# Four inner pairs instead of three in the gate_up groups of a fused encoder layer, with four raw buffers, five weight places and the residual's memory for summed blocks

## The chip, the cores and the metric

One core of a Trainium2 chip runs the whole layer as one program. The metric is the device time of one execution in microseconds (us). TensorE (PE) multiplies, VectorE (DVE) and ScalarE (ACT) prepare operands and finish results, GpSimd (POOL) and SyncE (SP) issue the DMAs; SP's queue and POOL's queue are each worked off in order.

## The reference, cut to what matters

```python
def swiglu(h, w_gate_up, w_down):
    gate, up = jnp.split(h @ w_gate_up, 2, axis=-1)
    return (jax.nn.silu(gate) * up) @ w_down

def reference(...):                      # x: 1 x 256 x 2048, float32; DEPTH = 1, D_FF = 5632
    ...                                  # four mixers side by side, w_out; x = x + mix @ w_out
    x = x + cross_attention(rms_norm(x, norm_g[l, 1]), mem_n, w_xq[l], w_xkv[l], w_xo[l])
    x = x + swiglu(rms_norm(x, norm_g[l, 2]), w_gate_up[l], w_down[l])
    return rms_norm(x, final_norm_g)
```

Everything is float32. The change lies in `swiglu`: h is 256 x 2048, `w_gate_up` 2048 x 11264, `w_down` 5632 x 2048.

## The kernel before, in words

**Products.** Each float32 operand is split into a high and a low part. A 128 x 512 block of a product is three matmuls (`part`, L430 to L434): high by high, high by low, low by high.

**The weight stream.** All weights lie in DRAM in the order in which they are used, as slabs of 1 MB (`Stream`). `_load` (L94) brings a slab into one of three raw buffers by a DMA on SP. `_half` (L112) turns half a slab (1024 columns) into a pair `wh`, `wl`: ACT casts (L135), DVE subtracts (L136). A pair takes a place (`_buffers`, L88): three places in pool `wp`, and a fourth, `extra`, over most of the program. `_fill` (L166) prepares as many halves ahead of TensorE as there are places.

**Normal and paired slabs.** A normal slab (N) is four steps of 128 inner rows by 512 columns, for two row blocks of the activations: 24 matmuls of 128 x 512. A paired slab (S) holds 256 inner rows by 1024 columns and does them with seven products instead of eight (`paired_rows`, `take_sums`): 21 matmuls. For that, two inner blocks of the activations are combined once (`combine`, into a tile `z`), and the weights are prepared in four pieces (`_sums`, L140): 1024 columns, 512, a summed block of 1024, 1024. DVE adds raw blocks for the last two (L158). In gate_up the summed block `two` is made partly by DMA: two loads of 256 KB on SP (L101) and one of 512 KB on POOL that adds on arrival (L102); then DVE has two adds of 512 columns left.

**The gate_up stage.** `gate_up` (L1047) walks over 11 groups of 512 hidden columns of gate and of up. Group 0 has eight normal slabs, in which the last blocks of h arrive and the combinations are made. Groups 1 to 10 follow the plan `NNSNSNSN`. After the last S of a group, `mixed` and `gated` read four and two PSUM banks; at the group's end `upped` reads the last two and `up` multiplies by the gate (L1060), transposes (L557) and stores the block to DRAM through POOL (L559). All eight banks are used by a group and pass to the next.

**Background work.** `Background` (L204) is a planner: at each step of TensorE's program, `poll` lets a waiting generator go on if its due time has come and the estimated DVE work that is owed is under 0.9 us. `fetch` (L1087) is one of these: it loads the stored hidden blocks k back from DRAM, turned (L564 on POOL, into the 11 tiles of pool `tmp`), and splits each into a tile `f[k]` (L290 on ACT, L282 on DVE). `early` is the fetch of blocks 0 to 21, begun in group 1; the rest follow after the stage. `bg.drain(early)` (L1135) puts down whatever of it is left before `down` begins. `down` (L1138) starts with four normal slabs, which use `f[12]` to `f[27]` in that order, and then alternates with paired slabs.

The framework puts the instructions of each engine into one fixed order when the program is built; each engine then works through its list in that order.

Of the kernel before, what the change touches and what calls it, by code (L numbers as in the profile page):

```python
# [13 lines left out]
F32 = mybir.dt.float32  # L14
F32R = mybir.dt.float32r
# [8 lines left out]
P = 128  # L24
R = 256
# [24 lines left out]
PAIRED = {a + i for a, plan in [(GATE_UP + 8 * j, GROUP) for j in range(10)] + [(DOWN, PASSES[0]), (DOWN + 22, PASSES[1])]  # L50
          for i, x in enumerate(plan) if x == "S"}
SUMMED = {i for i in PAIRED if i < DOWN}

# [18 lines left out]
class Stream:  # L72


    def __init__(self, tc, pools, W, bg):
        self.tc, self.nc, self.W, self.bg = tc, tc.nc, W, bg
        self.rawp, self.wp = pools
        self.order = []
        self.n = self.made = 0
        self.after = []  # L80
        self.halves = []
        self.at = self.phase = 0
        self.raw = None
        self.extra = self.sums = None
        self.places = []
        self.two = []

    def _buffers(self, n, m):  # L88
# [77 lines left out]
    def _fill(self):  # L166

        ahead = self.at + 1 + min(3 if self.extra else 2, self.n // 16)
        while len(self.halves) < ahead and self.made < NBLK:
            self._half()  # L170

    def _used(self):
# [81 lines left out]
class Block:  # L254
    def __init__(self, ctx, tc, t):
        self.ctx, self.tc, self.nc, self.t = ctx, tc, tc.nc, t
        pool = lambda n, b, **kw: ctx.enter_context(tc.tile_pool(name=n, bufs=b, **kw))
        self.cp = pool("cp", 1)
        self.tp = pool("tp", 11)
        self.rp = pool("rp", 3)  # L260
        self.psG = pool("psG", 4, space=PSUM)
        self.psM = pool("psM", 4, space=PSUM)
        rawp = pool("rawp", 3)
        wp = pool("wp", 3)
        self.bg = Background()
        self.st = Stream(tc, (rawp, wp), t["W"], self.bg)
        self.kept = itertools.count()
        self.run()

# [193 lines left out]
    def paired_rows(self, w, cols, slots, sums, plan, mixed, first, ready=None, late=0, before=None, swap=False):  # L463
# [23 lines left out]
        for i, kind in enumerate(plan):  # L487
            if before:
                before(i)
            if kind == "S":  # L490
                ks, z = next(todo)
# [75 lines left out]
    def run(self):  # L567
# [20 lines left out]
        self.ff = self.outside("hidden", FT)  # L588
        self.gk = [nc.dram_tensor(f"state{i}", (R, P), F32, kind="Internal").ap() for i in range(4)]
        self.vd = nc.dram_tensor("values", (P, 8 * 512), F32, kind="Internal").ap()  # L590
        def load(src, k, n):
# [16 lines left out]
        nc.scalar.copy(self.identr, self.ident)  # L608
        with self.tc.tile_pool(name="wx", bufs=1) as st.extra:
            self.attention(self.mixers())  # L610
# [199 lines left out]
    def half(self, c, r):  # L810

        return self.res[c].rearrange("p k r -> p (k r)")[:, r * 512:(r + 1) * 512]

    def turned(self, to, c, r, x):
# [52 lines left out]
    def attention(self, ps):  # L867
        tc, nc, act, st = self.tc, self.nc, self.act, self.st
        with tc.tile_pool(name="atp", bufs=1) as atp, tc.tile_pool(name="kp", bufs=1) as kp, \
# [109 lines left out]
            self.add_rows(1, 2, self.gemm_rows("w_xo", [1024], o)[0])  # L979
            late.append(self.bg.add(self.arrive(self.xf[1], 2, self.tmp, self.put3, FAR), go=True))  # L980
            st.extra = None
            self.add_rows(1, 3, self.gemm_rows("w_xo", [1536], o)[0])
            for g in late[:2]:
                self.bg.drain(g)
# [44 lines left out]
    def mlp(self):  # L1029
        tc, nc, act = self.tc, self.nc, self.act  # L1030
        with tc.tile_pool(name="fp", bufs=1) as fp:
            self.gap(fp, 192)
            f = [fp.tile([P, 512], F32R, name=f"f{i}") for i in range(14)]
            z = [fp.tile([P, 1024], F32R, name=f"z{i}") for i in range(3)]
            f = act[4:12] + f + [z[i // 2][:, i % 2 * 512:i % 2 * 512 + 512] for i in range(6)] + self.h3
            with tc.tile_pool(name="wy", bufs=1) as self.st.extra:
                self.gap(self.st.extra, 64)
                with tc.tile_pool(name="tw", bufs=2) as self.st.sums, tc.tile_pool(name="gp", bufs=1) as gp:
                    self.gate_up(gp, f, z)
# [7 lines left out]
    def gate_up(self, gp, f, z):  # L1047
# [65 lines left out]

        arrival = lambda: gp.tile([P, R], F32, name="ar", tag="ar", bufs=4)
# [9 lines left out]
        comb = self.bg.add(combined())  # L1124
        ps = self.gemm_rows("w_gate_up", [0, DFF], self.h3,
                            parts=[(range(8), [0]), (range(8, 12), [0]), (range(12), [1]), (range(12, 16), [0]), (range(12, 16), [1])],
                            before=lambda n: n in (1, 3) and self.bg.drain(self.late if n == 1 else last))
        self.bg.drain(col)
        gate(ps[0])
        up(0, ps[1])  # L1130
        early = self.bg.add(fetch(0, FT - 22, 3, 2.0, 15))
        self.bg.drain(comb)
        for j in range(1, DFF // 512):
            upped(j, self.paired_rows("w_gate_up", [j * 512, DFF + j * 512], self.h3, sums, GROUP, mixed, gated, swap=j % 2 == 0)[0])
        self.bg.drain(early)  # L1135
        self.fetch = self.bg.add(fetch(FT - 22, FT, 6, SOON))

    def down(self, f, sp):  # L1138
# [54 lines left out]
        for i, plan in enumerate(PASSES):  # L1193
# [5 lines left out]
            def before(j):  # L1199
                while plan[j] == "S" and len(made) <= plan[:j].count("S"):  # L1200
                    self.bg.step(next(e for e in self.bg.q if e[0] is g))
                if late and j == len(plan) - 2:
                    st.extra = None

# [686 lines left out]
```

## Time and profile before

| | |
|---|---|
| median of 3 runs | 1439.03 us (1435.91 to 1439.53) |
| the profiled execution: own time, span | 1434.72 us, 1432.9 us |
| granted TensorE clock | 0.998 |
| PE, DVE, ACT, POOL busy | 99%, 80%, 57%, 16% |
| gate_up groups 1 to 10 | some 41.5 us each, to 1192.8 us |

Busy PE is the time in which a matmul is under way, and matmuls overlap: a 128 x 512 one is shown with 389 ns, and the next starts 227 ns after it. Idle time of an engine is listed with what ended it. "L136" is a line of the kernel before.

### The profile page before, as it was taken

Reading aid. Unit: us, or ns where it says so; the run is one execution under the profiler, and the core shown is the slowest. Engines: PE = TensorE matmul, PEld = TensorE weight load, DVE = VectorE, ACT = ScalarE, POOL = GpSimd, SP = SyncE. Lnnn points to the kernel's source line nnn. Section 1 sums busy time; section 2 is a strip of 40 time slices with the busy share of each in tenths; the row PEclk is TensorE's granted clock in tenths of the full one; section 3 lists DMA queues with packets and bytes.
Section 4 is the critical chain, followed back from the end, with each engine's and each line's share of the span. In section 5 each row is a group of like instructions: output and inputs, shape, how many; then the busy total and the mean of one; then the engine's idle time right before and its main releaser. Section 6 shows DMA issues by size and latency. Waiting matters only on the chain.

```text
span 1432.9 us, 18653 instructions
## 1 busy us (share of the span) xinstructions
PE 1423.0 (99%) x6589; PEld 1181.4 (82%) x6589; DVE 1145.7 (80%) x1738; ACT 815.8 (57%) x1183; POOL 234.6 (16%) x306
## 2 busy tenths in 40 slices
PE   9999999999999999999999999999999999999997
PEld 8888888888888888888888888888888888788886
DVE  6667868777877767777677888889888888989997
ACT  7556565446745555556455556555555556655655
POOL 0000100013212223531430121122011002000000
PEclk9999999999999999999999999999999999999999
DMA  9877554456667787865986989899999887665554
GB/s 350 299 291 247 205 202 166 171 172 224 198 199 232 235 271 246 275 201 171 287 242 207 283 280 289 275 275 285 294 293 289 264 265 227 217 231 180 193 219 147
DMA packets 73038, 343.80 MB, mean 240 GB/s; under 512 B 10957, under 2 KB 12654, under 8 KB 45168
## 3 DMA queue, kind: packets, MB, share of 16 engines
q1 hardware_dynamic: 54848, 288.98, 57.6%
q0 software_dynamic: 17664, 52.97, 15.6%
q8 instruction: 51, 0.84, 0.2%
q10 hardware_dynamic: 432, 0.66, 0.1%
q14 instruction: 43, 0.35, 0.1%
HBM read 322.12 MB, written 20.45 MB: 239 GB/s over the span
## 4 chain that ended last, share of the span: by engine, by line
PE 98%; DVE 1%; DMA 0%; ACT 0%; issue 0%; SPq 0%; ACTq 0%
PE pg L432 22%; PE pg L433 22%; PE pg L434 22%; PE pm L432 7%; PE pm L434 7%; PE pm L433 7%; PE pg L380 4%; PE pg L381 2%; PE pm L1344 1%; PE pm L1022 1%; PE pm L993 1%; PE pm L1753 0%; DMA raw<-in_W 0%; DVE res L282 0%; PE pm L994 0%; PE pm L1518 0%
## 5 line engine op out<-in xcount | busy, mean ns | idle before, releaser
L136 DVE TENSOR_TENSOR wl<-raw,wh 128x1024 fp32r<-128x1024 f32 (+1 forms) x413 | 494.1, 1211 | 167.6 <-ACT wh L135 164.8
L135 ACT CAST wh<-raw 128x1024 fp32r<-128x1024 f32 (+1 forms) x413 | 424.7, 1043 | 282.9 <-PE pg L434 188.3
L432 PE MATMUL pg<-wh,act 128*128 128x512 f32 (+1 forms) x1191 | 465.5, 391 | 0.0
L433 PE MATMUL pg<-wl,act 128*128 128x512 f32 (+1 forms) x1191 | 463.9, 389 | 0.1
L434 PE MATMUL pg<-wh,act 128*128 128x512 f32 (+1 forms) x1191 | 463.8, 390 | 0.0
L432 PEld LDWEIGHTS pg<-wh,act 128*128 128x128 f32 x1191 | 224.0, 188 | 47.9 <-issue 1.5
L434 PEld LDWEIGHTS pg<-wh,act 128*128 128x128 f32 x1191 | 223.9, 188 | 47.5 <-DVE act L282 0.6
L433 PEld LDWEIGHTS pg<-wl,act 128*128 128x128 f32 x1191 | 224.0, 188 | 46.5 <-DVE wl L136 1.2
L147 ACT CAST wh<-raw 128x1024 fp32r<-128x1024 f32 (+1 forms) x150 | 137.4, 921 | 149.6 <-PE pg L434 53.8
L148 DVE TENSOR_TENSOR wl<-raw,wh 128x1024 fp32r<-128x1024 f32 (+1 forms) x150 | 155.9, 1060 | 52.8 <-ACT wh L147 52.6
L433 PE MATMUL pm<-wl,act 128*128 128x512 f32 x309 | 120.3, 389 | 0.1
L432 PE MATMUL pm<-wh,act 128*128 128x512 f32 x309 | 120.2, 389 | 0.0
L434 PE MATMUL pm<-wh,act 128*128 128x512 f32 x309 | 120.2, 389 | 0.0
L380 PE MATMUL pg<-act,wh 128*128 128x512 f32 x256 | 90.5, 395 | 0.0
L381 PE MATMUL pg<-act,wl 128*128 128x256 f32 x256 | 71.8, 280 | 0.0
L433 PEld LDWEIGHTS pm<-wl,act 128*128 128x128 f32 x309 | 58.0, 188 | 12.3 <-DVE wl L136 0.4
L434 PEld LDWEIGHTS pm<-wh,act 128*128 128x128 f32 x309 | 58.0, 188 | 12.1
L432 PEld LDWEIGHTS pm<-wh,act 128*128 128x128 f32 x309 | 58.0, 188 | 12.0
L102 POOL DMA_DIRECT2D two<-in_W x30 | 26.6, 885 | 237.6 <-DMA two<-in_W 106.4
L158 DVE TENSOR_TENSOR raw<-raw 128x512 f32<-128x512 f32 x90 | 61.8, 687 | 1.2
L147 ACT CAST wh<-two 128x1024 fp32r<-128x1024 f32 x30 | 31.5, 1051 | 52.0 <-PE pg L434 27.0
L380 PEld LDWEIGHTS pg<-act,wh 128*128 128x128 f32 x256 | 48.1, 188 | 10.5
(375 smaller groups left out, 1819.3 us busy)
## 6 DMA issues: line engine op xcount, KB each, us to landing
raw<-in_W SPq DMA_DIRECT2D x216, 1024.0 KB, 5.6
raw<-in_W SPq DMA_DIRECT2D x30, 768.0 KB, 6.3
two<-in_W SPq DMA_DIRECT2D x60, 256.0 KB, 4.8
two<-in_W POOLq DMA_DIRECT2D x30, 512.0 KB, 9.0
raw<-in_W SPq DMA_DIRECT2D x11, 512.0 KB, 7.1
hidden<-g POOLq DMA_DIRECT2D x22, 256.0 KB, 3.8
tmp<-hidden POOLq DMA_DIRECT2D x44, 128.0 KB, 6.0
features<-tmp POOLq DMA_DIRECT2D x32, 128.0 KB, 5.2
```

Source lines behind the costliest of these rows:

```text
L102: nc.gpsimd.dma_start(t, W[:, 512:1536], accum_op=ALU.add)
L135: nc.scalar.copy(wh[:, a:b], r[:, a:b])
L136: nc.vector.tensor_tensor(out=wl[:, a:b], in0=r[:, a:b], in1=wh[:, a:b].bitcast(F32), op=ALU.subtract)
L147: nc.scalar.copy(wh, src)
L148: nc.vector.tensor_tensor(out=wl, in0=src, in1=wh.bitcast(F32), op=ALU.subtract)
L158: nc.vector.tensor_tensor(out=out, in0=a, in1=b, op=ALU.add)
L380: self.nc.tensor.matmul(p[:, :], wh, slot[:, :], start=start, stop=False)
L381: self.nc.tensor.matmul(p[:, 0:R], wl, slot[:, 0:R], start=False, stop=stop)
L432: self.nc.tensor.matmul(p, hi, wh, start=start, stop=False)
L433: self.nc.tensor.matmul(p, hi, wl, start=False, stop=False)
L434: self.nc.tensor.matmul(p, lo, wh, start=False, stop=stop)
L993: nc.tensor.matmul(p[:, :], q[d][:, r * P:(r + 1) * P], kt[d][:, :], start=d == 0, stop=False)
```

## The change

- The plan of groups 1 to 9 is `NSSNSSNN` (four S, two of them in a row), that of group 10 `NSNSNSNN` (three S). There are four combined tiles `z` and 12 tiles of pool `fp` for `f` instead of three and 14; `f[20]` and `f[21]` lie in the memory of the tile that group 10 does without, and their splits wait for that group.
- The places are a list (`ring`): three of `wp`, `wx` in the first part, and in gate_up `wy` and `wz`, five in all. Raw buffers are a list as well (`raws`): three, and a fourth, `rawx`, from the end of group 0 to step 5 of group 10.
- The summed block is begun two slabs ahead of its use, not one: SP loads 256 KB once, ACT copies it to the other half of the tile (kept at its place in ACT's list), and POOL then issues the adding load. The four tiles for it are the residual's (`res`). The residual is written to DRAM by four stores of 512 KB (`leave`) and read back by four loads after group 10.

```diff
-GROUP = "NNSNSNSN"
+GROUPS = *["NSSNSSNN"] * 9, "NSNSNSNN"
...
+AHEAD = (-2, -2)
+SUMS = [{GATE_UP + 8 * j + i + a: GATE_UP + 8 * j + i for j in range(10) for i, x in enumerate(GROUPS[j % len(GROUPS)]) if x == "S"}
+        for a in AHEAD]
...
     def _buffers(self, n, m):
-        pool = self.extra if self.extra and len(self.halves) % 4 == 3 else self.wp
+        slot = min(self.ring, key=lambda x: x[1])
+        assert slot[1] < self.at or slot[1] < 0
+        pool, slot[1] = slot[0], len(self.halves)
...
     def _load(self, n):
-        self.raw = self.rawp.tile([P, 2048], F32, name="raw", tag="raw")
-        if n // 16 + 1 in SUMMED:
-            W, t = self.W[n // 16 + 1], self.sums.tile([P, 1024], F32, name="two", tag="two")
-            for a in (0, 512):
-                nc.sync.dma_start(t[:, a:a + 512], W[:, 1536:2048])
-            nc.gpsimd.dma_start(t, W[:, 512:1536], accum_op=ALU.add)
+        slot = min(self.raws, key=lambda x: x[1])
+        slot[1] = n
+        self.raw = slot[0].tile([P, 2048], F32, name="raw", tag="raw")
+        if n // 16 in SUMS[0]:
+            t = self.sums[0]
+            self.sums.append(self.sums.pop(0))
+            nc.sync.dma_start(t[:, 0:512], self.W[SUMS[0][n // 16]][:, 1536:2048])
+            self.begun.append(t)
+        if n // 16 in SUMS[1]:
+            t = self.begun.pop(0)
+            mark = len(nc.cur_bb.bb.instructions)
+            nc.scalar.copy(t[:, 512:1024], t[:, 0:512])
+            self.keep(mark)
+            nc.gpsimd.dma_start(t, self.W[SUMS[1][n // 16]][:, 512:1536], accum_op=ALU.add)
             self.two.append(t)
...
     def _fill(self):
-        ahead = self.at + 1 + min(3 if self.extra else 2, self.n // 16)
+        ahead = self.at + 1 + min(len(self.ring) - 1, self.n // 16)
...
+    def leave(self, c):
+        self.nc.sync.dma_start(self.rd[:, c * 1024:(c + 1) * 1024], self.whole(c))
...
-            f = [fp.tile([P, 512], F32R, name=f"f{i}") for i in range(14)]
-            z = [fp.tile([P, 1024], F32R, name=f"z{i}") for i in range(3)]
+            f = [fp.tile([P, 512], F32R, name=f"f{i}") for i in range(12)]
+            z = [fp.tile([P, 1024], F32R, name=f"z{i}") for i in range(4)]
...
                 if k >= k0 + ahead:
+                    while k0 == 0 and k - ahead >= 20 and "free" not in box:
+                        yield
...
-        sums = [((2 * i, 2 * i + 1), z[i]) for i in range(GROUP.count("S"))]
+        sums = [((2 * i, 2 * i + 1), z[(i + 1) % 4]) for i in range(4)]
...
+        rx = more.enter_context(self.tc.tile_pool(name="rawx", bufs=1))
+        self.st.raws.append([rx, -1])
...
         for j in range(1, DFF // 512):
+            plan = GROUPS[(j - 1) % len(GROUPS)]
+            if j == 10:
+                box["free"] = True
...
+        for c, x in enumerate(whole):
+            nc.sync.dma_start(x, self.rd[:, c * 1024:(c + 1) * 1024])
         self.bg.drain(early)
```

More of the change, by code (lines that the diff above doesn't have):

```diff
@@ L166, in _fill, with lend, back @@
     def _fill(self):
-        ahead = self.at + 1 + min(3 if self.extra else 2, self.n // 16)
+        ahead = self.at + 1 + min(len(self.ring) - 1, self.n // 16)
         while len(self.halves) < ahead and self.made < NBLK:
             self._half()
+    def lend(self, pool):
+        self.ring.append([pool, -1])
+        return pool
+    def back(self, *pools):
+        self.ring = [x for x in self.ring if x[0] not in pools]
+        self.raws = [x for x in self.raws if x[0] not in pools]
     def _used(self):
@@ L608, in run @@
         nc.scalar.copy(self.identr, self.ident)
[L609 removed]
+        with self.tc.tile_pool(name="wx", bufs=1) as self.wx:
+            st.lend(self.wx)
             self.attention(self.mixers())
@@ L979, in attention @@
             self.add_rows(1, 2, self.gemm_rows("w_xo", [1024], o)[0])
+            for c in range(2):
+                self.leave(c)
             late.append(self.bg.add(self.arrive(self.xf[1], 2, self.tmp, self.put3, FAR), go=True))
-            st.extra = None
+            st.back(self.wx)
             self.add_rows(1, 3, self.gemm_rows("w_xo", [1536], o)[0])
+            self.leave(2)
             for g in late[:2]:
@@ L1032, in mlp @@
             self.gap(fp, 192)
-            f = [fp.tile([P, 512], F32R, name=f"f{i}") for i in range(14)]
-            z = [fp.tile([P, 1024], F32R, name=f"z{i}") for i in range(3)]
[L1035 to L1038, printed above, removed]
+            f = [fp.tile([P, 512], F32R, name=f"f{i}") for i in range(12)]
+            z = [fp.tile([P, 1024], F32R, name=f"z{i}") for i in range(4)]
+            f = act[4:12] + f + [z[i // 2][:, i % 2 * 512:i % 2 * 512 + 512] for i in range(8)] + self.h3
+            with tc.tile_pool(name="wy", bufs=1) as self.wy:
+                self.gap(self.wy, 64)
+                self.st.lend(self.wy)
+                with tc.tile_pool(name="wz", bufs=1) as self.wz, tc.tile_pool(name="gp", bufs=1) as gp:
                     self.gate_up(gp, f, z)
@@ L1121, in combined, with before @@
                 yield from self.combine(z, *(self.h3[k] for k in ks))
-        sums = [((2 * i, 2 * i + 1), z[i]) for i in range(GROUP.count("S"))]
+        sums = [((2 * i, 2 * i + 1), z[(i + 1) % 4]) for i in range(4)]
         comb = self.bg.add(combined())
+        whole = [self.whole(c) for c in range(4)]
+        def before(n):
+            if n == 1:
+                self.st.lend(self.wz)
+                self.st.sums = list(whole)
+            if n in (1, 3):
+                self.bg.drain(self.late if n == 1 else last)
+            if n == 3:
+                self.leave(3)
         ps = self.gemm_rows("w_gate_up", [0, DFF], self.h3,
                             parts=[(range(8), [0]), (range(8, 12), [0]), (range(12), [1]), (range(12, 16), [0]), (range(12, 16), [1])],
-                            before=lambda n: n in (1, 3) and self.bg.drain(self.late if n == 1 else last))
+                            before=before)
         self.bg.drain(col)
+        arp.close()
+        more = ExitStack()
+        rx = more.enter_context(self.tc.tile_pool(name="rawx", bufs=1))
+        self.st.raws.append([rx, -1])
         gate(ps[0])
@@ L1133, in gate_up @@
         for j in range(1, DFF // 512):
-            upped(j, self.paired_rows("w_gate_up", [j * 512, DFF + j * 512], self.h3, sums, GROUP, mixed, gated, swap=j % 2 == 0)[0])
+            plan = GROUPS[(j - 1) % len(GROUPS)]
+            if j == 10:
+                box["free"] = True
+            upped(j, self.paired_rows("w_gate_up", [j * 512, DFF + j * 512], self.h3, sums[:8 - plan.count("N")], plan, mixed, gated,
+                                      before=lambda i: (j, i) == (10, 5) and self.st.back(self.wz, rx), swap=j % 2 == 0)[0])
+        more.close()
+        for c, x in enumerate(whole):
+            nc.sync.dma_start(x, self.rd[:, c * 1024:(c + 1) * 1024])
         self.bg.drain(early)
```

23 lines of the change are left out of this document (16 added, 7 removed).

## The prediction

> **What bounds the kernel now.** I read the page first: the busy times and the chain that ended last.
>
> ```profile
> PE 1423.0 (99%) x6589; PEld 1181.4 (82%) x6589; DVE 1145.7 (80%) x1738; ACT 815.8 (57%) x1183; POOL 234.6 (16%) x306
> PE 98%; DVE 1%; DMA 0%; ACT 0%; issue 0%; SPq 0%; ACTq 0%
> ```
>
> TensorE is the chain: 98% of the span, with nothing released late by another engine. So a matmul that is taken out is worth its own pitch, as long as nothing else becomes late. The pitch is read from TensorE's timeline at the end of gate_up:
>
> ```profile
> 1192.58 0.39 PE L434 MATMUL pm<-wh,act 128*128 128x512 f32 x1
> 1192.80 0.39 PE L432 MATMUL pg<-wh,f 128*128 128x512 f32 x1
> 1193.03 0.39 PE L433 MATMUL pg<-wl,f 128*128 128x512 f32 x1
> 1193.26 0.39 PE L434 MATMUL pg<-wh,f 128*128 128x512 f32 x1
> 1193.48 0.39 PE L432 MATMUL pg<-wh,f 128*128 128x512 f32 x1
> ```
>
> Three starts lie in 1193.48 - 1192.80 = 0.68 us: 0.227 us for a matmul. The operand changes from `act` to `f` with no gap: the first products of `down` follow the last of gate_up at once. A group of five N and three S has 183 matmuls, 41.5 us by this. Next, what the other engines have left in that time (busy time by stretches):
>
> ```profile
> core 0: us, PE busy (x) PEld busy (x) DVE busy (x) ACT busy (x) POOL busy (x), PEclk, DMA share, GB/s
> 773.00:818.00 45.00, 45.00 (x200) 37.28 (x199) 33.80 (x37) 23.47 (x26) 7.71 (x9) 1.00 0.78 240
> ...
> 860.00:902.00 42.00, 42.00 (x187) 34.76 (x187) 37.11 (x46) 24.08 (x29) 7.76 (x9) 1.00 0.94 289
> ```
>
> TensorE has no idle time, DVE 88% of the stretch busy, ACT 57%, the DMA engines 94%. DVE is the engine that can become the bound, and its rows in eight of these groups (818 to 1152 us, forms apart) give the prices:
>
> ```profile
> L136 DVE TENSOR_TENSOR wl<-raw,wh 128x1024 fp32r<-128x1024 f32 x81 | 95.8, 1216 | 6.5 <-ACT wh L135 5.6
> L148 DVE TENSOR_TENSOR wl<-raw,wh 128x1024 fp32r<-128x1024 f32 x48 | 58.6, 1222 | 32.2 <-ACT wh L147 32.1
> L148 DVE TENSOR_TENSOR wl<-two,wh 128x1024 fp32r<-128x1024 f32 x24 | 29.3, 1221 | 3.5 <-ACT wh L147 3.5
> L158 DVE TENSOR_TENSOR raw<-raw 128x512 f32<-128x512 f32 x24 | 16.5, 689 | 0.6
> L148 DVE TENSOR_TENSOR wl<-raw,wh 128x512 fp32r<-128x512 f32 x24 | 16.4, 683 | 0.0
> ...
> L282 DVE TENSOR_TENSOR f<-tmp,f 128x256 fp32r<-128x256 f32 x14 | 5.8, 417 | 0.0
> ...
> L282 DVE TENSOR_TENSOR act<-tmp,act 128x256 fp32r<-128x256 f32 x7 | 2.9, 417 | 0.0
> ```
>
> The last two rows are `fetch`: 21 of the 22 hidden blocks of `early` are split in these groups, one after another.
>
> **The saved matmuls.** Nine more S, each 21 matmuls instead of 24: 27 x 0.227 = 6.1 us less on the path. This term is sure.
>
> **What an S costs DVE.** An S takes 3 x 1.22 + 0.68 for its pieces and 2 x 0.69 for its adds, 5.7 us; an N takes 2 x 1.22 = 2.4. So a group has 3.3 us more. Now it has 36.7 in 41.5 us (37.1 x 41.5/42); with 40.0 in 40.8 us there would be hardly any slack.
>
> **Where `early` goes.** This is the step on which I rest most. `poll` lets `fetch` go on only while the estimated owed DVE work is under 0.9 us. With an S more and a fifth place, the planner's estimate stays above that: in the built program's order, groups 1 to 9 hold not one split of `early` any more. Three of them (blocks 0 to 2) stand in group 10, and the others behind that group's last transposes. So DVE has 8.7/8 = 1.1 us less per group, 38.9 of 40.8; and `down` begins with splits that aren't made. DVE's order there is: the two adds of `upped`, two multiplications, two transposes, then the splits of blocks 3 to 12, ten of them, and only block 12 is what TensorE's first step of `down` needs. Each engine works its list in order, so this is a sum. The rows of that place now:
>
> ```profile
> 1194.64 1.27 DVE L282 TENSOR_TENSOR h<-h,pm 128x512 f32<-128x512 f32 x2
> 1195.84 1.40 DVE L286 SCALAR_TENSOR_TENSOR h<-h,rc,g 128x512 f32<-128x512 f32 x2
> 1197.16 1.29 DVE L557 STREAM_TRANSPOSE g<-h 128x512 f32<-128x512 f32 x2
> 1198.38 3.45 DVE L136 TENSOR_TENSOR wl<-raw,wh 128x1024 fp32r<-128x1024 f32 x3
> ...
> 1203.43 0.76 DVE L282 TENSOR_TENSOR z<-tmp,z 128x256 fp32r<-128x256 f32 x2
> 1204.10 1.01 DVE L282 TENSOR_TENSOR tmp<-tmp 128x128 f32<-128x128 f32 x4
> ```
>
> The six operations take 1198.38 - 1194.64 = 3.74 us, and a split in a row of them (1204.10 - 1203.43)/2 = 0.335. Let T be the end of TensorE's group 10 (1192.80 in this trace). DVE began them 1.84 us after T here, because the last S is step 7 of 8; in the changed plan it is step 6, which gives DVE 5.4 us more, so I take T itself. Then block 12 is ready at T + 3.74 + 10 x 0.335 = T + 7.1. TensorE's list has four matmuls with its high part first (ACT is early with that), 0.9 us of work. Lost: 7.1 - 0.9 = **6.2 us**. From below, 5.5 (the first of the two banks is complete 0.68 us before T); from above, 8.0 (DVE as late as now).
>
> Block 14 comes next in question. Its load needs a `tmp` tile that block 3's split frees, and in POOL's order it stands behind the two stores of group 10:
>
> ```profile
> 1198.15 1.52 POOL L559 DMA_DIRECT2D hidden<-g  x2 [30.44 <-DVE g L557]
> ```
>
> ```profile
> DMA to landing us min/median/max: 3.6/6.5/7.7
> ```
>
> The second line is the landing of `tmp<-hidden` at this place. POOL is done with the stores at 1199.67, which is 1.29 after DVE's last transpose: T + 3.74 + 1.29 = T + 5.0. The load lands at T + 11.5, and ACT's cast (0.40, next fence) makes it T + 11.9. TensorE would take it at T + 7.1 + 0.45 + 1.36 = T + 8.9. Lost: **3.0 us**, between 0.1 and 4.2 by the landing's ends. The loads after it follow at 0.9 us, faster than TensorE uses blocks (1.36 us each), so I cost them at nothing; if they landed slower than that, each would cost the difference.
>
> **Two S in a row.** ACT's and POOL's part in the summed block:
>
> ```profile
> L147 ACT CAST wh<-two 128x1024 fp32r<-128x1024 f32 x24 | 25.2, 1052 | 39.7 <-PE pg L434 21.0 <-PE pm L434 18.7
> L147 ACT CAST wh<-raw 128x512 fp32r<-128x512 f32 x24 | 14.9, 620 | 13.1 <-PE pg L434 7.6 <-PE pm L434 5.4
> L1077 ACT ACTIVATE g<-g,rc 128x512 f32<-128x512 f32 x17 | 12.3, 722 | 3.3 <-DVE g L282 3.3
> L290 ACT CAST f<-tmp 128x256 fp32r<-128x256 f32 x14 | 5.6, 400 | 0.0
> ```
>
> ```profile
> DMA to landing us min/median/max: 6.8/9.6/10.9
> ```
>
> ```profile
> 912.38 1.22 DVE L148 TENSOR_TENSOR wl<-two,wh 128x1024 fp32r<-128x1024 f32 x1
> ...
> 915.39 1.23 DVE L148 TENSOR_TENSOR wl<-raw,wh 128x1024 fp32r<-128x1024 f32 x1 [0.86 <-ACT wh L147]
> ```
>
> The middle line is the landing of POOL's adding load in these groups. Before, POOL issued it as soon as SP's loads had landed; now ACT's copy stands between, at a fixed place in ACT's list. For the second S of a group, that list has: the cast of the first S's 512 piece, which needs a place that is free at S - 2.72 (S: the group's start; half of a slab is 12 matmuls), then the gate's activation, then the copy. That is S - 2.72 + 0.62 + 0.72 + 0.62 = S - 0.8; a landing of 9.6 makes S + 8.8. Then the cast of the summed piece (1.05) and, as the third fence shows from one start to the other's end, 916.62 - 912.38 = 4.24 us through add and cast to the last piece: S + 14.1. TensorE wants that piece at 5.44 + 4.76 + 3.4 = S + 13.6, its low part 0.2 later. So I take **0.3 us** a group, 2.7 in nine; by the landing's ends it is nothing, or 1.6 a group (14). The other three summed blocks of a group have 3 us or more to spare by the same sum.
>
> **What lies beside other work, at nothing.** The 39 copies on ACT: 0.62 each, ACT is at 57%; they cost only through the sum above. A fourth combination in group 0: some 3 us of DVE, which has 11 idle in 773 to 818. SP's bytes fall by 0.75 MB a group (an S needs 0.75 + 0.25 MB there instead of 1.25, an N 1.0). The residual's 4 stores and 4 loads of 512 KB on SP wait for data that is done by then, and nothing but weight slabs, a slab or more ahead, queues behind them; without that cover each costs a transfer, and the nearest row (512 KB) has 6.6 us:
>
> ```profile
> res<-in_xT SPq DMA_DIRECT2D x4, 512.0 KB, 6.6
> ```
>
> **The sum.** -6.1 + 6.2 + 3.0 + 2.7 = +5.8 us. Against the profiled execution's own 1434.72 us that is 1440.5. The median of the runs shown, 1439.03, is 0.3% above that execution; on it, 1444.8.
>
> **The rivals.**
>
> *The pairs run clean and the first load is quick (not slower).* The landing decides: below 9.3 us for the adding load nothing is lost in the groups, and at 3.6 us block 14 costs 0.1. Then -6.1 + 5.5 (or 6.2) + 0.1 (to 3.0) = -0.5 to +3.1, which is 1438.5 to 1442.1. For it: SP moves less, so landings may shorten, and the fetch loads are gone from the groups. Against it: 0.94 of DMA share now. It could be a gain beyond 0.3% only if the splits were hidden, against the order.
>
> *DVE becomes the bound of the groups.* 38.9 of 40.8 us leaves 1.9. But DVE's idle time in the first three rows above, 42 us in eight groups or 5.3 us each, is waiting for casts which wait for a place. If 60% of it stays in spite of the fifth place, a group lasts 38.9 + 3.2 = 42.1: 1.3 us a group over TensorE's time, 12 in nine; if all, 44.2 and 31. With 6.2 + 3.0 - 6.1 that is +15 to +34, 1454 to 1473. It decides from 36% on (1.9 of 5.3). For it: the bursts, two S in a row need 11.4 us of DVE in 9.5 of TensorE's. Against it: three N follow at the group's end.
>
> *The clock falls in the stall.* This trace shows a slow start:
>
> ```profile
> 1.07 4.64 PE L601 MATMUL pm<-ones 128*128 128x128 f32 x20 [1.07 <-DVE eps L602]
> ...
> 6.57 0.41 PE L434 MATMUL pg<-wh,act 128*128 128x256 f32 x1
> 6.79 0.37 PE L432 MATMUL pg<-wh,act 128*128 128x256 f32 x1
> 6.99 0.28 PE L433 MATMUL pg<-wl,act 128*128 128x256 f32 x1
> 7.11 0.28 PE L434 MATMUL pg<-wh,act 128*128 128x256 f32 x1
> ```
>
> Until 6.9 us the 256-wide matmuls follow at 0.21, then at 0.12: nearly double. If the stall puts TensorE back into that state for the 5.9 us from its first matmul to the full rate, half of that is lost: +2.9 on the sum, 1447.7. Against it: the four early matmuls cut the wait in two, and block 14's wait would hide some of it. [...]
>
> **How the numbers follow.** The forecast has 0.45, its own range is +2 to +11 (1441 to 1450); clean pairs 0.28; DVE as the bound 0.17; the clock 0.10. What can be told from no change is about 0.3%, 4.3 us. Faster by more than that: 0.07, for a gain that I don't see. Within it: most of the clean case and the lower end of the forecast, 0.31. Slower: 0.62. The range that leaves out 2 in 10 goes from a little under the clean case into the lower third of the DVE case: 1437 to 1459.
>
> **What would show it.** TensorE's timeline at the end of gate_up should have a gap of some 6 us in all before the third product of `f`, and then one before the third block; DVE's timeline there ten splits in a row after two transposes; DVE's rows between group 2 and 9 no `f<-tmp`. The groups should last 40.8 to 41.3 us. Wrong I would be if the splits stand inside the groups, if no wait longer than 2 us follows the last transposes, or if the groups last over 42 us.

## The result, and the profile after

The changed kernel takes 1462.21 us (median of four runs, 1456.4 to 1463.82) against 1437.66 (1435.91 to 1439.53) for the kernel before beside it: a ratio of 1.0163, 95% interval 1.0131 to 1.0195. The profiled execution has 1461.85 us of its own and a span of 1460.1, 27.1 us more than before. The forecast was +5.8 with a range of 1437 to 1459, so the direction was right and the size was not: the time lies above the range.

The page after, busy times and the chain that ended last:

```profile
PE 1430.9 (98%) x6562; PEld 1176.1 (81%) x6562; DVE 1173.0 (80%) x1782; ACT 848.3 (58%) x1242; POOL 242.4 (17%) x315
PE 72%; issue 11%; DMA 7%; DVE 6%; ACT 2%; POOL 2%; SPq 0%; POOLq 0%; ACTq 0%; DVEq 0%
```

TensorE has its 27 instructions less, and yet the chain leaves it for 28% of the span (2% before). Where it waits is read from TensorE's timeline, stage by stage: the start of each group (the bank changes there), T (the end of group 10), ACT's copy into `u` in the middle of `down`, and the last matmul ("after `u`" ends there; from it to the end of the span after takes 0.7 us less than before, so that a row need not add up to the own times exactly). Groups of four S are held against 180 x 0.2267 = 40.81 us, groups of three against 41.49. In us, each run's profiled execution against that of before; "up to 690" is the same work in all of them and shows how far two executions differ by themselves.

| run | own time | up to 690 | 690 to group 1 | groups 1 to 10, over TensorE's pace | T to `u` | after `u` | matmuls saved |
|---|---|---|---|---|---|---|---|
| before | 1434.72 | 0 | 0 | 0.0 | 0 (102.2) | 0 | 0 |
| after | 1461.85 | +0.7 | +2.6 | +15.9 | +14.2 | +0.7 | -6.1 |
| forecast | 1440.5 | | 0 | +2.7 | +9.2 | 0 | -6.1 |

The ten groups after take 44.2, 43.7, 45.3, 42.5, 41.2, 41.2, 41.3, 40.9, 42.9 and 41.5 us. Groups 5 to 8 are what was forecast; 1 to 4 and 9 are not. TensorE's waits between 786 and 1170 us (engine and line, what released it, total, times, longest):

```profile
PE pm L460 <- DVE wl L166: 3.0, 4, 0.8
PE pg L460 <- DVE wl L166: 2.3, 3, 0.8
PE pm L459 <- ACT wh L165: 2.1, 4, 1.4
PE pg L459 <- ACT wh L165: 0.5, 2, 0.3
```

All of these are waits for pieces of paired slabs (L165 and L166 are `_sums`; L135, L136 and L147, L148 of before are L153, L154, L165, L166 now). What stands behind them shows in group 3 (869.1 to 914.4 us), in the chain of waits of that stretch:

```profile
874.45 0.78 POOL hidden L586
875.23 8.12 DMA hidden<-g
...
885.40 0.87 POOL tmp L591
886.27 10.37 DMA res<-in_W
...
896.74 1.05 ACT wh L165
897.79 0.02 issue
897.82 1.24 DVE wl L166
899.05 0.04 issue
899.09 0.50 PE pm L460
```

POOL's list has three loads of `early` (`tmp<-hidden`, L591) ahead of the adding load for the group's fourth S. They wait for the stores of the hidden block to land (8.12 us); only then is the adding load issued, 17.2 us into the group (12.9 to 13.2 in groups 5 to 8), and it lands 10.4 us later. In groups 1 and 2 it is issued 1 to 2 us late, and beside these loads it takes 11.7 and 12.1 us to land instead of 9.0 to 10.7. In group 9 there is no such load, and the place of ACT's copy does it. ACT's timeline in group 9 (starts at 1121.5) and in group 7 (1039.3):

```profile
1131.88 1.05 ACT L153 CAST wh<-raw 128x1024 fp32r<-128x1024 f32 x1 [1.59 <-PE pg L461]
1133.24 1.05 ACT L153 CAST wh<-raw 128x1024 fp32r<-128x1024 f32 x1 [0.31 <-PE pg L461]
1134.19 1.05 ACT L165 CAST wh<-raw 128x1024 fp32r<-128x1024 f32 x1
1135.14 0.61 ACT L118 COPY res<-res 128x512 f32<-128x512 f32 x1
...
1146.87 1.05 ACT L165 CAST wh<-res 128x1024 fp32r<-128x1024 f32 x1 [2.64 <-DMA res<-in_W]
```

```profile
1051.35 0.62 ACT L118 COPY res<-res 128x512 f32<-128x512 f32 x1
1051.87 1.99 ACT L153 CAST wh<-raw 128x1024 fp32r<-128x1024 f32 x2
...
1063.04 1.06 ACT L165 CAST wh<-res 128x1024 fp32r<-128x1024 f32 x1 [1.02 <-DMA res<-in_W]
```

In groups 4 and 9 two normal casts stand ahead of the copy in ACT's list, and the second waits for a place. The copy comes 13.6 us into the group, not 12.1, and the cast of the summed piece 25.4, not 23.7. At 23.7 the group loses 0.5, at 25.4 it loses 2.1, and at 27.6 (group 3) 4.5: by these three, from some 23.3 us on, each us late costs one. In groups 5 to 8 the block lands 22.2 to 23.6 us into the group, so even the best of them had only about 1 us to spare.

The boundary is as the prediction has it. TensorE's and DVE's timelines (T = 1205.85):

```profile
1207.54 0.50 PE L459 MATMUL pg<-wh,f 128*128 128x512 f32 x1 [1.53 <-ACT f L317]
1207.88 0.40 PE L460 MATMUL pg<-wl,f 128*128 128x512 f32 x1
1208.12 0.40 PE L459 MATMUL pg<-wh,f 128*128 128x512 f32 x1
1208.36 0.40 PE L460 MATMUL pg<-wl,f 128*128 128x512 f32 x1
1212.80 1.22 PE L461 MATMUL pg<-wh,f 128*128 128x512 f32 x2 [4.04 <-DVE f L309]
1213.82 0.63 PE L459 MATMUL pg<-wh,f 128*128 128x512 f32 x1
1214.25 0.63 PE L460 MATMUL pg<-wl,f 128*128 128x512 f32 x1
...
1217.23 0.40 PE L461 MATMUL pg<-wh,f 128*128 128x512 f32 x1
1217.47 0.40 PE L459 MATMUL pg<-wh,f 128*128 128x512 f32 x1
```

```profile
1208.12 1.30 DVE L584 STREAM_TRANSPOSE g<-h 128x512 f32<-128x512 f32 x2
1209.34 1.72 DVE L309 TENSOR_TENSOR act<-tmp,act 128x256 fp32r<-128x256 f32 x5
1210.98 2.10 DVE L309 TENSOR_TENSOR f<-tmp,f 128x256 fp32r<-128x256 f32 x6
```

Two transposes, then the splits in a row, and the third product of `f` at T + 6.95 (T + 7.1 was forecast). Behind the wait the matmuls follow at 0.427 us instead of 0.227: the granted clock is 0.50 from 1210.4 to 1217.2 us, partly in the wait itself.

The last loss lies ahead of the groups, and the forecast has nothing there. SP's timeline after, the cast that waits, and SP's timeline of run e7 (below) at the same place:

```profile
715.18 0.33 SPq L847 DMA_DIRECT2D residual<-res  x1
721.02 0.33 SPq L113 DMA_DIRECT2D res<-in_W  x1
721.75 17.43 SPq L126 DMA_DIRECT2D raw<-in_W  x4
```

```profile
734.25 2.94 ACT L153 CAST wh<-raw 128x1024 fp32r<-128x1024 f32 x3 [6.02 <-DMA raw<-in_W]
```

```profile
704.57 39.60 SPq L129 DMA_DIRECT2D raw<-in_W  x8
744.22 0.44 SPq L114 DMA_DIRECT2D res<-in_W  x1
```

A store of the residual (L847) waits on SP for DVE. Behind it stands the first load of a summed block into that tile (L113), which waits for the store to land: the framework had moved it far ahead of its use. No weight slab is issued from 711 to 721.75 us, and TensorE waits twice behind 736 us, together 2.4 us (from start to start, less the pitch of 0.227).

### The profile page after: what moved, and what is told of

It is laid out like the page before. It is cut to its first block, busy times and chain, and to the rows that moved or that the text cites. A ratio compares the mean times of both kernels' runs of the same rounds, so it can differ in the third digit from the quotient of the medians.

```text
span 1460.1 us, 18662 instructions
## 1 busy us (share of the span) xinstructions
PE 1430.9 (98%) x6562; PEld 1176.1 (81%) x6562; DVE 1173.0 (80%) x1782; ACT 848.3 (58%) x1242; POOL 242.4 (17%) x315
## 4 chain that ended last, share of the span: by engine, by line
PE 72%; issue 11%; DMA 7%; DVE 6%; ACT 2%; POOL 2%; SPq 0%; POOLq 0%; ACTq 0%; DVEq 0%
PE pg L460 17%; PE pg L459 17%; PE pg L461 16%; PE pg L407 4%; PE pm L460 4%; PE pm L461 4%; PE pm L459 4%; DMA raw<-in_W 3%; DMA res<-in_W 2%; PE pg L408 2%; DVE wl L154 2%; DVE wl L166 1%; PE pm L1409 1%; DMA hidden<-g 1%; ACT wh L153 1%
## 5 line engine op out<-in xcount | busy, mean ns | idle before, releaser
L154 DVE TENSOR_TENSOR wl<-raw,wh 128x1024 fp32r<-128x1024 f32 (+1 forms) x395 | 474.3, 1213 | 163.8 <-ACT wh L153 161.6
L153 ACT CAST wh<-raw 128x1024 fp32r<-128x1024 f32 (+1 forms) x395 | 406.4, 1041 | 258.1 <-PE pg L461 183.8
L459 PE MATMUL pg<-wh,act 128*128 128x512 f32 (+1 forms) x1165 | 455.9, 392 | 1.7 <-ACT wh L153 1.6
L460 PE MATMUL pg<-wl,act 128*128 128x512 f32 (+1 forms) x1165 | 454.4, 390 | 2.3 <-DVE wl L154 2.3
L461 PE MATMUL pg<-wh,act 128*128 128x512 f32 (+1 forms) x1165 | 454.0, 390 | 0.9 <-DVE act L309 0.9
L459 PEld LDWEIGHTS pg<-wh,act 128*128 128x128 f32 x1165 | 219.2, 188 | 50.1 <-ACT wh L153 3.6
L461 PEld LDWEIGHTS pg<-wh,act 128*128 128x128 f32 x1165 | 218.8, 188 | 47.1 <-DVE act L309 1.5
L165 ACT CAST wh<-raw 128x1024 fp32r<-128x1024 f32 (+1 forms) x177 | 160.5, 918 | 162.5 <-DVE raw L176 66.1
L166 DVE TENSOR_TENSOR wl<-raw,wh 128x1024 fp32r<-128x1024 f32 (+1 forms) x177 | 182.7, 1059 | 37.5 <-ACT wh L165 37.1
L460 PE MATMUL pm<-wl,act 128*128 128x512 f32 x290 | 113.2, 390 | 0.2 <-DVE wl L154 0.2
L461 PE MATMUL pm<-wh,act 128*128 128x512 f32 x290 | 112.9, 390 | 0.0
L459 PE MATMUL pm<-wh,act 128*128 128x512 f32 x290 | 112.6, 390 | 0.0
L120 POOL DMA_DIRECT2D res<-in_W x39 | 34.8, 892 | 308.3 <-ACT res L118 239.5
L176 DVE TENSOR_TENSOR raw<-raw 128x512 f32<-128x512 f32 x99 | 68.2, 689 | 0.6
L460 PEld LDWEIGHTS pm<-wl,act 128*128 128x128 f32 x290 | 54.5, 188 | 12.1 <-DVE wl L154 0.7
L459 PEld LDWEIGHTS pm<-wh,act 128*128 128x128 f32 x290 | 54.4, 188 | 11.4 <-ACT wh L153 0.2
L461 PEld LDWEIGHTS pm<-wh,act 128*128 128x128 f32 x290 | 54.5, 188 | 11.2
L165 ACT CAST wh<-res 128x1024 fp32r<-128x1024 f32 x39 | 41.1, 1054 | 32.0 <-DMA res<-in_W 19.0
L407 PEld LDWEIGHTS pg<-act,wh 128*128 128x128 f32 x256 | 48.2, 188 | 10.4
```

The lines of the kernel that those rows point to most:

```text
L120: nc.gpsimd.dma_start(t, self.W[SUMS[1][n // 16]][:, 512:1536], accum_op=ALU.add)
L153: nc.scalar.copy(wh[:, a:b], r[:, a:b])
L154: nc.vector.tensor_tensor(out=wl[:, a:b], in0=r[:, a:b], in1=wh[:, a:b].bitcast(F32), op=ALU.subtract)
L165: nc.scalar.copy(wh, src)
L166: nc.vector.tensor_tensor(out=wl, in0=src, in1=wh.bitcast(F32), op=ALU.subtract)
L176: nc.vector.tensor_tensor(out=out, in0=a, in1=b, op=ALU.add)
```

## The experiments

Theory: the groups lose because the fourth summed block lands late, by its places in POOL's and ACT's lists, and `down` loses because of the splits behind the last transposes. The rival is the one of the prediction whose range held the result: DVE is the bound of the groups (1454 to 1473). The last columns of the table, for all runs:

| run | ratio to before, 95% interval | own time | 690 to group 1 | groups | T to `u` |
|---|---|---|---|---|---|
| e1 begun three slabs ahead | 1.0091 (1.0076 to 1.0106) | 1448.80 | +4.8 | +3.3 | +12.4 |
| e2 loads of `early` in group 6 | 1.0154 (1.0137 to 1.0171) | 1457.12 | +2.6 | +12.8 | +12.0 |
| e3 splits forced into the groups | 1.0175 (1.0159 to 1.0190) | 1460.41 | +4.6 | +23.8 | +3.1 |
| e4 = e1 and e3 | 1.0051 (1.0036 to 1.0066) | 1444.03 | +3.0 | +8.7 | +2.8 |
| e5 before, splits kept back | 1.0073 (1.0058 to 1.0088) | 1447.74 | +0.1 | +0.4 | +11.8 |
| e6 after, TensorE kept busy | 1.0175 (1.0158 to 1.0191) | 1462.58 | +5.7 | +13.9 | +14.3 |
| e7 = e4, stores on POOL's queue | 1.0034 (1.0020 to 1.0049) | 1441.84 | +1.3 | +8.8 | +2.7 |
| e8 three S, new memory, begun as e1 | 1.0019 (1.0010 to 1.0029) | 1438.77 | +3.8 | -0.1 | -0.1 |
| e9 = e7, other places for the splits | 1.0051 (1.0038 to 1.0065) | 1443.70 | +0.2 | +10.6 | +3.3 |
| e10 four S in six groups | 0.9984 (0.9975 to 0.9993) | 1436.75 | +1.2 | +3.2 | +0.6 |
| e11 = e8, stores on POOL's queue | 0.9991 (0.9982 to 1.0000) | 1435.62 | +0.1 | -0.1 | +0.4 |
| e12 = e7, old order in group 10 | 1.0029 (1.0018 to 1.0041) | 1439.93 | +0.6 | +8.2 | +2.8 |

**e1: the summed block begun earlier**

```diff
-AHEAD = (-2, -2)
+AHEAD = (-3, -3)
```

> The summed block is begun three slabs ahead of its use instead of two (AHEAD = (-3, -3)); nothing else changes. ACT's copy for the group's fourth S then stands some 8 us earlier in ACT's list. Late landing (the fourth summed block arrives after TensorE wants it, because ACT's copy and POOL's queue release its adding load late): groups 1 to 4 and 9, which take 44.2, 43.7, 45.3, 42.5 and 42.9 us in the changed kernel, come down to 40.8 to 41.3 and the time falls by 12 to 15 us, to an own time of 1447 to 1450. DVE as the bound of the groups: DVE has the same work, the groups stay as they are, 0 to -2 us. By both the gap behind group 10 stays.

Measured: 1448.80 us of its own, 13.05 less than after, as expected of a late landing; the nine groups of four S take 41.0 to 41.3 us each. TensorE's waits between 788 and 1160 us are an empty list. DVE is no less busy than before the edit: group 3 of after, and a group of e1 (columns: busy time of PE, PEld, DVE, ACT and POOL, clock, DMA share):

```profile
869.00:914.40 45.40, 43.26 (x183) 34.50 (x182) 38.02 (x46) 26.12 (x31) 8.01 (x10) 0.96 0.88 254
```

```profile
988.50:1029.70 41.20, 41.20 (x181) 33.64 (x180) 37.84 (x45) 26.40 (x31) 5.10 (x6) 1.00 0.89 268
```

The same 38 us of DVE fit into 41.2 us. DVE is not the bound; the landing was. What stays is 0.36 us a group: in most, gaps of some 0.2 at the low part of the last piece of the second or the fourth S. They don't come from a landing. In e1 the fourth block lands 10 to 16 us into the group, and its cast begins at 22.7 to 22.9 all the same (22.9 in the group from 988.5 us), behind a cast that waits for TensorE to free a place:

```profile
1010.74 0.62 ACT L165 CAST wh<-raw 128x512 fp32r<-128x512 f32 x1 [0.32 <-PE pm L461]
1011.41 1.06 ACT L165 CAST wh<-res 128x1024 fp32r<-128x1024 f32 x1
```

**e2: the loads of `early` moved**

```diff
-                    while len(stored) <= k // 4:
+                    while len(stored) <= k // 4 or k0 == 0 and "go" not in box:
...
+                    if k0 == 0 and k < 11:
+                        self.keep_place(mark)
...
-        early = self.bg.add(fetch(0, FT - 22, 3, 2.0, 15))
+        early = self.bg.add(fetch(0, FT - 22, 10, 2.0, 15))
...
+            if (j, i) == (6, 4):
+                box["go"] = True
+                self.bg.step(entry)
```

> The first loads of the stored hidden blocks (early) are put at one place, group 6 behind the issue of the fourth summed block, instead of groups 1 to 3; the splits stay at the end of the stage. POOL's queue as the cause in groups 1 to 3: these lose 1.5 us together instead of 10.8, so -9.3 us (own time about 1452.5), while groups 4 and 9, where two normal casts stand ahead of ACT's copy, keep their 1.7 and 2.1, and group 6 loses nothing. If ACT or DVE alone make the block late: no change, 0 to -2.

Measured: groups 1 to 3 take 41.4, 41.1 and 40.9 us (44.2, 43.7, 45.3 after); groups 4 and 9 keep their 42.8 and 42.9. So POOL's queue made the first. For the second the place of ACT's copy is what is left; e1 moves it earlier and the loss goes, but moves SP's and POOL's part with it. Only 4.7 us came of e2, not 9.3: groups 6 and 7 now take 43.4 and 45.4. The twelve loads take POOL from 1003.6 to 1019 us, and in the chain of waits of that stretch a weight slab that SP issues right behind them takes 13.12 us to land (medians of this run: 5.2 for 1 MB, 6.6 for 768 KB):

```profile
1020.60 13.12 DMA raw<-in_W
...
1042.83 0.50 PE pm L460
```

The expectation that group 6 loses nothing was wrong: the loss went with the loads.

**e3 and e4: the splits forced into the groups**

```diff
+            if j > 2 and i in (0, 3, 7) and getattr(self, "have", 0) < (20 if j < 10 else 22) and entry in self.bg.q:
+                have = getattr(self, "have", 0)
+                for _ in range(3):
+                    if getattr(self, "have", 0) == have and entry in self.bg.q:
+                        self.bg.step(entry)
```

> The splits of early are forced into groups 3 to 10, three steps of the planner a group, instead of standing behind the last transposes. Ten splits in front of block 12: the stretch from the end of group 10 to the fourth paired slab of down loses at most 1.5 us instead of 14.2 (10.5 at the boundary with the half-rate clock in it, 3.7 after it), so -13. Its price: the loads of early now stand in POOL's list in groups 3 to 10 too; if POOL's queue makes the fourth block late, groups 4 to 8 lose 1 to 3 us each, together +5 to +12. DVE as the bound: all groups from 3 on last 42.1 us or more, +8 or more. Total -13 to 0; its parts are read by stage.

> Both edits together: summed blocks begun three slabs ahead and the splits of early forced into groups 3 to 10. If late landings and the held-back splits are the whole cause and DVE has room: -25 to -28, own time 1434 to 1437, groups at 40.8 to 41.5. If DVE becomes the bound with the splits in the groups (38.9 and more of 40.8 us busy): groups 3 to 9 last 42.1 to 44.2 and the time is 1444 to 1460.

Measured: in both the gap is gone, `f` follows T with no wait, and T to `u` falls from +14.2 to +3.1 and +2.8 (at most 1.5 expected of e3). In e3 the groups take it back (+23.8 for +15.9): the loads now stand in POOL's list in groups 4 and 5 too, where the fourth adding load is issued 16.8 and 15.6 us into the group (14.6 and 13.2 in after). With the block begun earlier (e4) the price is 5.4 (8.7 for e1's 3.3), and groups 3 to 9 take 41.1 to 43.1 us, 41.8 in the mean; DVE as the bound asks for 42.1 or more in each, and two of the seven reach that. The own time, 1444.03, missed its 1434 to 1437: the 5.4, and 3.0 ahead of the groups and 2.8 in `down`, had not been counted there. By the number alone it is at the lower end of what was expected of DVE as the bound (1444 to 1460). The longest wait in e4's groups is 1.3 us, in group 5; ACT waits 5.9 us for a weight slab ahead of it, and DVE is busy for 40.8 of that group's 43.0 us. So with the splits DVE still had room in the mean, but not at every place: behind a late slab it can't catch up at once.

**e5: the kernel before, with its splits kept back**

```diff
                 if k >= k0 + ahead:
+                    while k0 == 0 and "free" not in box:
+                        yield
...
+            if j == 10:
+                box["free"] = True
```

> The kernel before, with the splits of early kept back until group 10 and nothing else changed (three S, three places and a fourth, old summed blocks). In its list six splits then stand between the last two transposes and block 12, instead of none. If the held-back splits alone make the gap: the gap opens without the fourth S, T + 1.84 + 3.74 + 6 x 0.335 = T + 7.6 less 0.9 of work = 6.7 us, with the half-rate clock behind it 8 to 10 us in all, own time 1443 to 1445, and the groups stay at 41.5. If they are hidden by something else: 0 to +2.

TensorE's timeline at its boundary (T = 1194.03):

```profile
1195.35 0.50 PE L432 MATMUL pg<-wh,f 128*128 128x512 f32 x1 [1.16 <-ACT f L290]
...
1202.44 1.22 PE L434 MATMUL pg<-wh,f 128*128 128x512 f32 x2 [5.89 <-DVE f L282]
1203.46 0.63 PE L432 MATMUL pg<-wh,f 128*128 128x512 f32 x1
```

The gap opens without a fourth S, with the half rate behind it (the granted clock is 0.50 from 1202 to 1206 us), and costs 11.8 to `u` (8 to 10 expected; own time 1447.74, 1443 to 1445 expected). The third product comes at T + 8.4, not 7.6, mostly because DVE begins the six operations at T + 2.5 instead of T + 1.84.

**e6: TensorE kept busy in the wait**

```diff
+        warm = 24 * (w == "w_down" and not swap)
...
+            for _ in range(warm):
+                self.nc.tensor.matmul(q[name][:, :], self.h3[0][:, 0:P], wh, start=True, stop=True)
```

> The changed kernel with 24 products of 128x512 that nobody uses, put on TensorE ahead of the first step of down (5.4 us of work in the 7 us in which it waits); they write the bank that the first real product overwrites. If the long wait is what halves the clock: no half-rate stretch behind the boundary, the boundary loses 8.5 us instead of 10.5, -1.5 to -2.2 in all. If the half rate has another cause, or costs nothing in the end because DVE is late behind it: 0.

```profile
1206.74 5.60 PE L512 MATMUL pg<-wh,act 128*128 128x512 f32 x24
...
1213.68 0.73 PE L461 MATMUL pg<-wh,f 128*128 128x512 f32 x2 [0.43 <-DVE f L309]
...
1216.37 0.50 PE L459 MATMUL pg<-wh,f 128*128 128x512 f32 x1 [0.58 <-ACT f L317]
...
1218.68 0.50 PE L459 MATMUL pg<-wh,f 128*128 128x512 f32 x1 [0.65 <-ACT f L317]
```

No half rate: with TensorE at work in the wait, the granted clock is 1.00 from 1206 to 1244 us, where the changed kernel has 0.50 from 1210.4 to 1217.2. But nothing is won: waits for the loads of blocks 14 and 15 appear that the slow clock had covered, and by `u` the time from T is +14.3 for +14.2. So the half rate at this place cost nothing in the end.

**e7: the stores off SP's queue**

```diff
-        self.nc.sync.dma_start(self.rd[:, c * 1024:(c + 1) * 1024], self.whole(c))
+        self.nc.gpsimd.dma_start(self.rd[:, c * 1024:(c + 1) * 1024], self.whole(c))
...
+            if n // 16 < GATE_UP + 4:
+                self.keep(mark)
```

> The kernel of run e4 with the residual's four stores on POOL's queue instead of SP's, and the first group's loads into the residual's tiles kept at their place in SP's list instead of ahead of it. If SP's list (a store that waits for DVE, then a load that waits for that store's landing, with weight slabs behind both) makes the wait of 2.5 to 3.6 us at 730 us: that wait goes, -2.5 to -3.5 against e4, own time 1440 to 1441.5. If the 2 MB of stores themselves are the cost: 0 to -1.

> As e8 (three S everywhere, new memory), with the stores on POOL's queue and the first loads into the residual's tiles kept at their place. e8 loses 4.9 us ahead of group 1 and nothing else of size. If SP's list makes that: own time 1435 to 1437, -2 to -4 against e8. If the fourth combination in group 0 makes it (it is still made): 0 to -1.

e7 is 2.2 us under e4 (2.5 to 3.5 expected), and e11 3.2 under e8 (own times). The wait at 736 us is gone from both, with the same 2 MB stored: it was SP's list. Which of the two edits did it, the stores' new queue or the loads' place, was not tested apart. Where it is there, the stretch up to group 1 costs 2.6 to 5.7 us.

**e8 to e12: what a fourth S is worth**

One line each: the plan of e8 and e11, the condition of e9 in the place of e3's, the plan of e10, the plan of e12.

```diff
+GROUPS = ["NNSNSNSN"]
...
-            if j > 2 and i in (0, 3, 7) and getattr(self, "have", 0) < (20 if j < 10 else 22) and entry in self.bg.q:
+            if j > 1 and i in (6, 7) and getattr(self, "have", 0) < (20 if j < 10 else 22) and entry in self.bg.q:
...
+GROUPS = ["NSSNSSNN", "NSSNSSNN", "NSSNSSNN", "NNSNSNSN", "NNSNSNSN", "NNSNSNSN", "NSSNSSNN", "NSSNSSNN", "NSSNSSNN", "NNSNSNSN"]
...
+GROUPS = *["NSSNSSNN"] * 9, "NNSNSNSN"
```

> The new memory (four raw buffers, five places, summed blocks in the residual's tiles, begun three slabs ahead) with the old plan of three S in every group. It does 27 matmuls more than the changed kernel, none more than the kernel before. If the fourth S is what keeps the splits of early out of the groups: they stand in groups 2 to 8, no gap behind group 10, groups at 41.5 to 41.7, and only the wait at 730 us and a little in down is left: own time 1438 to 1442, +3 to +7 on before. If the new memory itself costs more in the groups: 1445 or above.

> As e7, but the splits of early are forced in at the two normal slabs that end each of groups 2 to 9 instead of at three steps of groups 3 to 9. e7's groups lose 8.1 us over TensorE's time, 3.3 of them as in e1 and 4.8 with the splits. If the place of the splits makes the 4.8: -2 to -4, own time 1438 to 1440. If DVE's room is used up wherever they stand: 0 to +3.

> Summed blocks begun three slabs ahead and stores on POOL's queue, as in e7, no forced splits; four S in groups 1 to 3 and 7 to 9, three S in the others, where the planner then places the splits by itself (groups 4 to 7, three in group 10). If a fourth S is worth 0.68 less the 0.36 that e1's groups still lose, and the planner's own places cost nothing: -1.9 for six, +1.6 ahead of group 1 as in e7, nothing behind group 10: own time 1434 to 1436, no difference from before that can be told. If the mixed order costs in the groups: 1438 or above.

> As e7, with the order of the kernel before, NNSNSNSN, in group 10 alone (it has three S in both). In every run with NSNSNSNN there, the first four paired slabs of down lose 2.4 to 2.8 us that the runs with the old order don't, also where no split is late. If group 10's order makes that: -2 to -2.8 against e7, own time 1439 to 1440. If the fourth S in the groups before it makes it: 0 to -0.5.

e8: with three S the planner puts the splits into the groups itself (groups 1 to 6); no gap, groups at TensorE's pace (a wait of 0.7 us three matmuls into group 1 is counted ahead of it). So the new memory costs nothing there, and the fourth S keeps the splits out. e9: 1.9 us worse than e7, not better. That is what was expected if DVE's room is used up wherever the splits stand (0 to +3). The longest wait in its groups, 2.3 us in group 5, ends a chain through ACT's and DVE's lists that has no landing in it from 935 us on. So of the places tried for the splits beside a fourth S, none is free. e12: its own time, 1439.93, is inside the expected 1439 to 1440, but not for the expected reason: T to `u` stays at +2.8, so group 10's order is not its cause, and the 1.9 us lie in group 10 itself and ahead of group 1. It stands in the five runs with forced splits (e3, e4, e7, e9, e12) and not where the planner puts them into the groups by itself (e8, e10, e11); its cause was not followed further. e10 is the fastest of all: four S where no split is due, three where they are. It is 0.16% under the kernel before, with an interval that leaves 1 out (median 1434.41; the profiled execution of the table has 1436.75). Against e11, which has the new memory and three S everywhere, its median is 1.0 us less: of the 4.1 us that its 18 matmuls save, the groups lose 3.2 again.

## Why the prediction was right and wrong

- **-6.1, the saved matmuls:** right, 27 instructions less.
- **+6.2, block 12's split:** right in each step. T + 6.95 for T + 7.1, splits in a row behind two transposes, no split in groups 2 to 9. What was short is the rest: T to `u` cost 14.2 where 9.2 stood. e5 shows that late splits alone do it (11.8). The wait itself is 5.9 of the 14.2 and the half rate behind it some 2 (ten matmuls at 0.427 us instead of 0.227). DVE then has to make the other splits beside `down`'s own pieces, and until it has caught up TensorE is held again and again: six gaps of 0.5 to 1.0 us from 1224 to 1280, 4.0 together, each ended by DVE. The forecast counted the delay of block 12 and not the DVE work that it puts off.
- **+3.0, block 14's load:** the issue came at T + 5.2 (T + 5.0), but the cast began at T + 9.3, since the load took 4.1 us, near the lower end of the row. By then the half-rate clock covered it; e6, without that cover, has 0.58 us of idle time there and 0.65 at the next block.
- **+2.7, two S in a row:** this is where the prediction failed. For the second S its size was right, partly by luck: groups 5 to 8 lose 0.1 to 0.5, but the second block landed 5.3 to 7.7 us into the group from group 2 on, not at 8.8, and its cast began at 7.7 or 7.8, so no landing cost anything there. The step that failed is the sentence behind it: "The other three summed blocks of a group have 3 us or more to spare by the same sum." For the fourth that sum, which is not written out, left out POOL's queue ahead of the adding load (the loads of `early`, up to 4.2 us late in groups 1 to 3) and took ACT's copy at one place for all groups (in groups 4 and 9 it stands behind a cast more). Even without these the spare time was about 1 us, not 3. The term was 15.9, and e1 brought it to 3.3.
- **At nothing, the residual's stores:** wrong by 2.6. That "nothing but weight slabs, a slab or more ahead, queues behind them" was no cover: three raw buffers don't hold the 10 us for which SP stood still, and the first load into the tile stood behind the store too.
- **Rivals.** DVE as the bound gave 1454 to 1473 and so holds the time, by another mechanism: e1 takes the groups' loss away with DVE's work unchanged. Only once the splits stand in the groups too (e4, e9) does DVE's list hold TensorE at single places. The half clock did happen behind the stall (0.50 from 1210.4 to 1217.2 us), and e6 shows that without it the time is the same (T to `u` +14.3 for +14.2). The splits were not hidden, as the order said.
- **The test named beforehand**, that the prediction is wrong "if the groups last over 42 us", struck: five of ten do.

## What to carry to other kernels

A step that is issued by one engine and waited for by another has a slack in each list that it passes, and the smallest one counts: follow every such block through all queues, and through all repeats, since an order that a program has made differs from one repeat to the next. Work that is put off does not only come late, it comes on top of the next stage's work. A store that waits in front of loads on one queue can hold them for longer than its own transfer takes: in the profile after, SP issued no weight slab from 711 to 721.75 us, and the residual's stores took 3.0 to 5.8 us to land.

## What the runs showed of the hardware

Half rate also came behind shorter waits than those at T in after (gaps of 1.69 and 4.21 us; gaps are from start to start, less one pitch). One gap of 2.3 us (e2 at 1042.8 us) was followed, 1.5 us later, by 8 matmuls at 0.39 to 0.43 (the granted clock is 0.72 in the mean of 1042 to 1048 us). Two gaps of 1.55 and 1.02 us in group 3 of after, up to 897.84 and 899.09 us, were followed by a granted clock of 0.50 from 899.79 to 903.20. Two of 1.15 and 1.22 us at 737 us (after) were not, with the clock at 1.00 from 735 to 745 us, nor 1.53 and 1.22 there (e4). The sum of the two gaps does not tell these apart (2.57 in group 3, 2.75 in e4); what does was not shown.

The table by stretches has group 3 of after (the fall comes at 899.79) and e4 (no fall; columns as above; the busy time counts a matmul by its shown length, so it is somewhat more than by the pitch):

```profile
896.38:899.79 3.41, 1.26 (x5) 0.80 (x5) 2.52 (x3) 1.59 (x3) 0.00 (x0) 1.00 0.40 169
899.79:903.20 3.41, 3.41 (x9) 2.07 (x8) 2.39 (x3) 3.41 (x5) 0.00 (x0) 0.50 0.43 100
```

```profile
733.75:737.16 3.41, 2.04 (x10) 1.38 (x8) 1.03 (x1) 2.11 (x3) 0.00 (x0) 1.00 0.70 269
737.16:740.58 3.42, 2.48 (x10) 1.82 (x11) 3.42 (x6) 2.18 (x3) 0.00 (x0) 1.00 0.01 2
```

The low rate lasted 3.41 us in group 3 of after and 6.83 us behind T (1210.40 to 1217.23 us), where TensorE still waited until 1212.8 us.

One wait cost more than its listed length: the matmul at 899.09 us in group 3 of after, which the profile lists with 0.76 us of idle time, starts 1.03 us later than it would have. The idle time is counted from the shown end of the matmul before, 0.50 us behind its start, where the next would have started after 0.227.
